# A trunk layer's first attention units: a PSUM strip for the scans, one projection bank, and stores behind the copies

## The chip, the cores and the metric

The kernel runs on one core of a Trainium2 chip. The metric is the device time of one execution in microseconds (us). In the profile PE is TensorE's matmul, PEld its weight load, DVE is VectorE, ACT ScalarE, POOL GpSimd; SP is the engine whose queue issues nearly all DMAs.

## What is computed

One decoder layer on x of 2048 tokens by 1024 features, float32: RMSNorm and a modulation by shift and scale, one input projection, attention on 16 heads of 64 (8 "stick-breaking", 8 "forgetting"), a per-head norm, an output projection, a gated residual, a gated MLP with a causal convolution, and a final RMSNorm. The change lies in the stick-breaking heads:

```
z = q.k / 8                      for s < t (strict)
A[t,s] = sigmoid(z_ts) * prod_{s<j<t} (1 - sigmoid(z_tj))
o = A v
```

The product runs from the diagonal back to s = 0, so a row of A is a running product read from right to left.

## The kernel before, in words

Tokens go in four blocks of 512 (`tb`), heads in pairs (`p`). A *unit* is one kind, one pair and one block; `units` lists 16 stick-breaking units and then 16 forgetting ones. Each unit has a projection (`proj_gen`, a generator advanced step by step by `fill_proj`) and an attention part (`attend`). Every float32 operand is split into a high part (ACT copy) and a low part (subtraction on DVE or POOL, `split`), and a product is three matmuls.

The first four units (pair 0, blocks 0 to 3) also normalise and modulate x. `first_block` does block 0; `norm_proj` does blocks 1 to 3 through `modulate`: four ACT squares (L95), a square root, four DVE multiplications (L108), then for each of eight feature tiles four PE transposes (L114), an affine step `hf`, and the split into `hp`. Each `hp` tile is stored to DRAM as `hs` (L433, 512 KB each) for the later pairs, which load it again (L321). A q accumulator `aq` and a k accumulator `ak` take 24 matmuls each (L252) in banks of tag `pj`, which has two banks in this stretch. `finish_proj` evacuates q (L262, L263) and k, copies them into `Q` and `K` by eight DMAs on SP (L266, L278), and makes V in four banks of 24 matmuls each (L247), of the same tag.

Attention part `SbItem.weights` makes the logits in PSUM (L442, L443), two sigmoids on ACT (L531 into `r`, L532 into `a`), a scan of `r` from right to left on DVE, and a multiplication on POOL (L546). `Group.turn` transposes the result and splits it (L457, L461, L462), `Group.add` multiplies it with V (L472). A row is cut into chunks of 512 keys, the last chunk first. The last chunk's scan (L538) stops products at the diagonal by a strip of constants, `edge`. Other chunks take the running product of the chunk to their right.

For units 0 to 2, `long_rows` is false. There each chunk has a tile of its own: POOL copies the neighbour's leftmost column into column `need` (L543) and the scan (L545) runs over 513 columns with initial value 1.0, both its inputs being `r` in SBUF. `edge` is read from SBUF. From unit 3 on, `long_rows` is true: pool `psa` is closed and opened again, one of its two banks becomes `edge_bank`, an ACT copy of `edge` into PSUM (L906), and tag `pj` has one bank; scans read that PSUM bank as second input and take the neighbour's column as the initial value (L541).

All loops are unrolled. The order on each engine is made by the framework's scheduler from the program order and modelled times; `tc.issue_after(ins)` keeps the instructions traced in its block behind `ins` on its engine. Attention of unit u stands in the program behind the projection of unit u, and between its steps stand those of projection u+1. x of block 1 is loaded in `first_block`, of block 2 behind `hs` of block 0 (L425), of block 3 when its projection starts. The list `first_done` holds instructions behind which the next `modulate` puts its squares and multiplications; before, only unit 0 fills it.

Of the kernel before, what the change touches and what calls it, by code (L numbers as in the profile page):

```python
# [11 lines left out]
AF = mybir.ActivationFunctionType  # L12
ALU = mybir.AluOpType
# [20 lines left out]
def kernel(ctx: ExitStack, tc: tile.TileContext, x, c, w_ada, b_ada, g_attn, w_in, b_fgate,  # L34
# [5 lines left out]
    def f(t):  # L40
        return t.bitcast(F32)
# [109 lines left out]
    def bank(pool, tag, bufs):  # L151
        return pool.tile([P, 512], F32, name=f"ps_{tag}", tag=tag, bufs=bufs)

    pj = lambda: bank(psa, "pj", 1 if edge_bank is not None else 2)
    qk = lambda: bank(psb, "qk", 2)
    pt = lambda: bank(psb, "pt", 3)
    pv = lambda: bank(psb, "pv", 1)
# [96 lines left out]
    def finish_proj(kind, p, tb, aq, w, hts, res, ak=None, avs=()):  # L254
        i = units.index((kind, p, tb))
        more = 3 < i < 16
        Q = ex.tile([P, 2, 2, TB], F32R, name="Q") if more and i % 3 == 2 else sb.tile([P, 2, 2, TB], F32R, name="Q", bufs=2)
        K = ex.tile([P, 2, TB], F32R, name="K") if i in (5, 13) else sb.tile([P, 2, TB], F32R, name="K", bufs=5)
        V = sb.tile([P, 4, 2, P], F32R, name="V", bufs=6)
        q2 = sl_.tile([P, 2, TB], F32R, name="q2", bufs=2)  # L260
        k2 = sl_.tile([P, 2, TB], F32R, name="q2", bufs=2)
        nc.scalar.activation(q2[:, 0], aq, AF.Copy, scale=-HD ** -0.5)  # L262
        nc.vector.scalar_tensor_tensor(q2[:, 1], aq, -HD ** -0.5, f(q2[:, 0]), ALU.mult, ALU.subtract)  # L263
        for h in range(2):
            for r in range(2):
                nc.sync.dma_start(f(Q[r * HD:(r + 1) * HD, h]), f(q2[h * HD:(h + 1) * HD]))  # L266
        if ak is None:
            ak = pj()
            for kt in range(KT):
                accumulate(ak, 1, w[0], hts[kt], kt)  # L270
                if kt % 2:
                    yield
        evacuated = split(k2[:, 0], k2[:, 1], ak, nc.vector)
        if i == 0:
            first_done.extend(evacuated)
        for h in range(2):
            for r in range(2):
                last_copy[:] = [nc.sync.dma_start(f(K[r * HD:(r + 1) * HD, h]), f(k2[h * HD:(h + 1) * HD, r])).ins]  # L278
        yield
        spill = vs[kind][p // 2][tb]  # L280
        if p % 2:
            nc.sync.dma_start(f(V), spill)
        else:
            V1 = (ex.tile([P, 4, 2, P], F32R, name="V") if (kind, p) == ("sb", 2) else
                  sb.tile([P, 4, 2, P], F32R, name="V", bufs=6))
            forget = (kind, p) == ("sb", 0)
            step, width = (1, 2 * P + NH) if forget else (2, 2 * P)
            if forget:
                zn = px.tile([P, 4, NH], F32, name="zn", bufs=1)
            for i in range(0, 4, step):  # L290
                if i < len(avs):
                    av = avs[i]
                else:
                    av = pj()
                    for t in range(step):
                        for kt in range(KT):
                            accumulate_v(av[:, t * width:(t + 1) * width], w[1], hts[kt], kt, i + t)
                            if kt % 4 == 3:
                                yield
                if forget:  # L300
                    nc.vector.tensor_copy(zn[:, i], av[:, 2 * P:width])
                av = av[:, 0:step * 2 * P].rearrange("p (t e h d) -> p t e h d", t=step, e=2, h=2)
                for e, v in enumerate((V, V1)):
                    v = v[:, i:i + step]
                    split(v[:, :, :, 0:HD], v[:, :, :, HD:P], av[:, :, e], nc.vector)
            if forget:
                b = pt()
                nc.tensor.transpose(b[0:4 * NH, 0:P], zn.rearrange("p t n -> p (t n)"), ident)
                zt = px.tile([4 * NH, P], F32, name="zt", bufs=1)
                nc.scalar.activation(zt, b[0:4 * NH, 0:P], AF.Identity, bias=bf_c)  # L310
                nc.sync.dma_start(zs[tb], zt)
            nc.sync.dma_start(spill, f(V1))
        res.append((Q, K, V))
        yield

# [19 lines left out]
    def first_block(xts, w, res):  # L335

        keep = tc.keep_in_program_order
        base = 3 * 512
        aq, ak = pj(), pj()
        avs = [qk(), qk(), pt()]  # L340
        junk = junk_x()
        for xt in xts:
# [28 lines left out]
        for kt in range(KT + 1):  # L371
# [42 lines left out]
            if kt + 1 < KT:  # L414
                with behind_last():
                    turned.append(turn(kt + 1))
        second_x.extend(load_x(1, keep))
        for t in range(4):
            keep(nc.sync.dma_start(bf_c[t * NH:(t + 1) * NH], b_fgate.rearrange("o n -> n o")))
        yield  # L420
        yield from finish_proj("sb", 0, 0, aq, w, hts, res, ak, avs)
        with tc.issue_after(last_copy[0]):
            for kt in range(KT):
                nc.sync.dma_start(hs[0][kt], f(hts[kt]))
            second_x.append(load_x(2))  # L425

    def norm_proj(tb, xts, w, res):
        aq = pj()
        hts = []

        def done(kt, h):
            hts.append(h)
            nc.sync.dma_start(hs[tb][kt], f(h))  # L433
            accumulate(aq, 0, w[0], h, kt)

        yield from modulate(px, pt, xts, mod_a, lambda kt: h_tile(), done, "a", nc.vector if tb == 1 else None, tb > 1,
                            junk_x())
        yield from finish_proj("sb", 0, tb, aq, w, hts, res)

    def logits(cw, qcols, hl, Q, K):  # L440
        b = qk()
# [60 lines left out]
    class SbItem:  # L502
# [14 lines left out]
        def weights(self, qi):  # L517
            head, ch = self.head, self.ch
            last = ch == head.n - 1
            need = min(512, (2 * head.j + qi + 1) * P - ch * 512)  # L520
            b = logits(max(need, 2 * P), head.qcols(qi), head.hl, head.Q, head.K[ch])
            if last:
                head.right = getattr(head, "right", [None, None])
                if long_rows:
                    head.right[qi] = sx.tile([P, S + 1], F32, name="rw", bufs=3)
            if long_rows:
                r = head.right[qi][:, ch * 512:ch * 512 + need + 1]
            else:
                r = sx.tile([P, 512 + 1], F32, name="r", bufs=7)
            self.at[qi] = a = sx.tile([P, 512], F32, name="a", bufs=7)  # L530
            nc.scalar.activation(r[:, :need], b[:, :need], AF.Sigmoid)  # L531
            nc.scalar.activation(a[:, :need], b[:, :need], AF.Sigmoid, scale=-1.0)  # L532
            if last:

                nc.gpsimd.memset(r[:, need:need + 1], 0.0)
                rev = r[:, 0:need][:, ::-1]
                strip = edge if edge_bank is None else edge_bank
                nc.vector.tensor_tensor_scan(rev, rev, strip[:, TB - need:TB][:, ::-1], 0.0, ALU.mult, ALU.max)  # L538
            elif long_rows:
                rev = r[:, 0:need][:, ::-1]  # L540
                nc.vector.tensor_tensor_scan(rev, rev, edge_bank[:, 0:need], r[:, need:need + 1], ALU.mult, ALU.bypass)  # L541
            else:
                nc.gpsimd.tensor_copy(r[:, need:need + 1], head.right[qi][:, 0:1])  # L543
                rev = r[:, 0:need + 1][:, ::-1]
                nc.vector.tensor_tensor_scan(rev, rev, rev, 1.0, ALU.mult, ALU.bypass)  # L545
            nc.gpsimd.tensor_mul(a[:, :need], a[:, :need], r[:, 1:need + 1])  # L546
            if not long_rows:
                head.right[qi] = r
# [204 lines left out]
        nc.vector.scalar_tensor_tensor(mod_m[:, 0], mod_m[:, 0], 1.0, cols[:, R_GM:R_GM + KT], ALU.add, ALU.mult)  # L753
        yield

    second_x = []
    last_copy = []
    units = [(k, p, tb) for k in ("sb", "fox") for p in range(4) for tb in range(NTB)]
    weights = {}
# [2 lines left out]
    def proj_gen(u, xts=None):  # L762
        kind, p, tb = u
        if tb == 0:
            weights[kind, p] = load_w(kind, p)
            results[kind, p] = []
        if u == units[0]:
            return first_block(xts, weights[kind, p], results[kind, p])
        if (kind, p) == ("sb", 0):
            return norm_proj(tb, second_x[:4] if tb == 1 else second_x[4] if tb == 2 else load_x(tb), weights[kind, p], results[kind, p])  # L770
        return proj(kind, p, tb, weights[kind, p], results[kind, p])

    HT = 2 * P
# [102 lines left out]
        yield from proj_gen(units[i], xt0 if i == 0 else None)  # L876

    psc = p2a = ex = edge_bank = None
    wo = []
    stock = [unit_proj(i) for i in range(len(units))]  # L880
    taken = [0]
# [18 lines left out]
    ex = open_pool("ex", side="right")  # L900
    sx = open_pool("sx", side="right")
    long_rows = True
    close_pool("psa")
    psa = open_pool("psa", side="right", space=PSUM)
    edge_bank = bank(psa, "edge", 1)
    nc.scalar.activation(edge_bank, edge[:, 0:TB], AF.Copy)  # L906
    base = taken[0]
    goal = 0
    seen = {}
# [11 lines left out]
        fill_proj(taken[0] + 1)  # L921
    close_pool("sx", "ex", "psa")
    ex = edge_bank = None
    psa = open_pool("psa", side="right", space=PSUM)
    sx = open_pool("fx", side="right")
    base = taken[0]
# [372 lines left out]
```

## Time and profile before

| what | value |
|---|---|
| median of 3 runs | 3098.84 us |
| the runs | 3099.03, 3098.84, 3090.37 us |
| the profiled execution's own time | 3090.19 us |
| its span | 3088.4 us |
| mean granted clock | 0.986 of full speed |
| PE busy | 2952.4 us, 96% |
| DVE, ACT, POOL busy | 2069.8, 1652.2, 1205.9 us |

The span is from the first to the last instruction; 1.8 us lie around it. A row of the windows view gives for one stretch its length and then busy us and instructions of each engine, the granted TensorE clock (1.00 is full speed), the share of time in which the 16 DMA engines were busy (rounded estimates can pass 1), and GB/s. A row grouped by line and form gives line, engine, operation, out<-in, shapes and count, then busy us, mean ns of one | idle us before the group and what ended it.

### The profile page before, as it was taken

What the parts mean: (1) busy time and instruction counts of PE and PEld (TensorE: products, weight loads), DVE (VectorE), ACT (ScalarE), POOL (GpSimd) and SP (SyncE); (2) the same over time, 40 slices, a digit from 0 to 9 for tenths busy, and PEclk for the clock granted to TensorE, in tenths of its full rate; (3) what the DMA queues carried; (4) which work ended last, traced back from release to release, by engine and by line L of the source; (5) the groups of instructions that cost most, each with busy time, mean ns of one, the idle gap of its engine ahead of it and who ended that gap; (6) DMA issues with size and microseconds to landing.
All of it is one profiled execution on the core that took longest, in us unless ns stands there. A gap on an engine that the chain in (4) does not pass through costs nothing.

```text
span 3088.4 us, 46309 instructions
## 1 busy us (share of the span) xinstructions
PE 2952.4 (96%) x15966; PEld 2507.9 (81%) x15966; DVE 2069.8 (67%) x3416; ACT 1652.2 (53%) x3041; POOL 1205.9 (39%) x1443
## 2 busy tenths in 40 slices
PE   6889999999999999999989899999899999999998
PEld 5778798989788888988878688888678888888887
DVE  5776788878856775657733777778977777254253
ACT  5665777767755655566634444444544444343332
POOL 1563655556531332242122344444444442332331
PEclk9999999999999999999999999999999999999999
DMA  8648634565166875595457532223332223565562
GB/s 234 214 137 266 194 116 148 179 198 164 26 221 219 292 225 176 177 329 133 155 188 231 186 90 82 82 82 89 113 95 82 83 82 114 196 199 167 183 205 79
DMA packets 292811, 496.51 MB, mean 161 GB/s; under 512 B 29336, under 2 KB 177552, under 8 KB 291552
## 3 DMA queue, kind: packets, MB, share of 16 engines
q1 hardware_dynamic: 280944, 480.92, 49.4%
q10 hardware_dynamic: 11632, 12.63, 1.2%
q8 instruction: 126, 2.06, 0.3%
q14 instruction: 109, 0.89, 0.1%
HBM read 352.61 MB, written 90.51 MB: 143 GB/s over the span
## 4 chain that ended last, share of the span: by engine, by line
PE 18%; DVE 10%; POOL 7%; DMA 7%; issue 5%; ACT 2%; SPq 1%; POOLq 0%; ACTq 0%; DVEq 0%
PE ps_o L1238 8%; PE ps_t L1238 4%; PE ps_bc L1238 4%; DMA wuraw<-in_w_up_dram 4%; DVE wu L45 3%; PE ps_o L1065 2%; POOL ws L1053 2%; POOL wuraw L1052 2%; DVE u L1134 2%; POOL ws L1051 2%; DMA hm<-hf_m 1%; DMA r<-rstd 1%; DVE u L1166 1%; DVE u L1133 1%; ACT wu L44 1%
## 5 line engine op out<-in xcount | busy, mean ns | idle before, releaser
L1065 PE MATMUL ps_o<-oa,wu 128*128 128x512 f32 x2088 | 504.5, 392 | 12.6 <-DVE oa L45 7.1
L1065 PEld LDWEIGHTS ps_o<-oa,wu 128*128 128x128 f32 x2088 | 391.1, 189 | 104.8 <-DVE oa L45 11.5
L472 PE MATMUL ps_pv<-at,V 128*128 128x256 f32 x2304 | 433.0, 298 | 13.9 <-DVE at L462 6.2
L462 DVE TENSOR_TENSOR at<-ps_pt,at 128x512 fp32r<-128x512 f32 (+1 forms) x576 | 365.4, 651 | 118.4 <-ACT at L461 115.7
L252 PE MATMUL ps_pj<-hp,w_qk 128*128 128x512 f32 x1536 | 417.4, 404 | 20.9 <-DMA hp<-hs 9.6
L461 ACT ACTIVATE at<-ps_pt 128x512 fp32r<-128x512 f32 (+1 forms) x576 | 319.2, 580 | 161.4 <-PE ps_pt L457 122.1
L472 PEld LDWEIGHTS ps_pv<-at,V 128*128 128x128 f32 x2304 | 340.3, 191 | 47.5 <-DVE at L462 14.8
L546 POOL TENSOR_TENSOR a<-a,rw 128x512 f32<-128x512 f32 (+2 forms) x272 | 262.8, 969 | 233.8 <-DVE rw L541 97.7
L252 PEld LDWEIGHTS ps_pj<-hp,w_qk 128*128 128x128 f32 x1536 | 277.2, 190 | 79.3 <-DMA hp<-hs 13.0
L45 DVE TENSOR_TENSOR wd<-wide,wd 128x1024 fp32r<-128x1024 f32 x88 | 117.3, 1339 | 249.6 <-ACT wd L44 227.5
L442 PE MATMUL ps_qk<-K,Q 128*128 128x512 f32 (+2 forms) x640 | 259.9, 407 | 16.0 <-ACT a L532 9.6
L45 POOL TENSOR_TENSOR g<-graw,g 128x512 fp32r<-128x512 f32 x82 | 139.3, 1702 | 296.8 <-ACT g L44 290.2
L1238 PE MATMUL ps_o<-wd,g 128*128 128x512 f32 x1040 | 249.3, 389 | 0.1
L1065 PE MATMUL ps_t<-ob,wu 128*128 128x512 f32 x984 | 242.0, 390 | 1.0 <-ACT hf_m L964 1.0
L443 PE MATMUL ps_qk<-K,Q 128*128 128x512 f32 (+2 forms) x640 | 237.1, 371 | 0.0
L44 ACT ACTIVATE wu<-wuraw 128x512 fp32r<-128x512 f32 x214 | 133.0, 626 | 184.1 <-PE ps_o L1065 115.3
L541 DVE TENSOR_TENSOR_SCAN rw<-rw,ps_edge 128x512 f32<-128x512 f32 x168 | 211.5, 1269 | 26.0 <-ACT rw L531 25.0
L1238 PEld LDWEIGHTS ps_o<-wd,g 128*128 128x128 f32 x1040 | 195.2, 188 | 41.1 <-DVE y L1184 0.5
L1065 PEld LDWEIGHTS ps_t<-ob,wu 128*128 128x128 f32 x984 | 184.9, 188 | 40.2 <-ACT hf_m L964 1.2
L247 PE MATMUL ps_pj<-w_v,hp 128*128 128x256 f32 (+1 forms) x1464 | 215.8, 289 | 0.7 <-DVE q L263 0.6
L247 PEld LDWEIGHTS ps_pj<-w_v,hp 128*128 128x128 f32 x1464 | 194.7, 191 | 7.0 <-DVE q L263 1.0
L457 PE MATMUL ps_pt<-edge,a 128*128 128x128 f32 x1088 | 183.8, 276 | 13.3 <-POOL a L546 6.2
(246 smaller groups left out, 5694.2 us busy)
## 6 DMA issues: line engine op xcount, KB each, us to landing
hp<-hs SPq DMA_DIRECT2D x224, 512.0 KB
wuraw<-in_w_up_dram SPq DMA_DIRECT2D x84, 512.0 KB
wide<-in_w_down_dram SPq DMA_DIRECT2D x84, 512.0 KB
Q<-q SPq DMA_DIRECT2D x128, 256.0 KB
g<-u SPq DMA_DIRECT2D x42, 512.0 KB
graw<-g SPq DMA_DIRECT2D x82, 256.0 KB
K<-q SPq DMA_DIRECT2D x128, 128.0 KB
hs<-hp SPq DMA_DIRECT2D x32, 512.0 KB
```

Source lines behind the costliest of these rows:

```text
L45: return [a.ins, (lo_engine or nc.gpsimd).tensor_sub(lo, src, f(hi)).ins]
L247: nc.tensor.matmul(acc, h[:, a, tok], w[kt][:, bb, 0:acc.shape[1]], start=kt == 0 and m == 0, stop=kt == KT - 1 and m == 2)
L252: nc.tensor.matmul(acc, w[kt][:, a, n], h[:, bb], start=kt == 0 and i == 0, stop=kt == KT - 1 and i == 2)
L442: nc.tensor.matmul(b[:, :cw], Q[:, hl, 0, qcols], K[:, hl, :cw], start=True, stop=False)
L443: nc.tensor.matmul(b[:, :cw], Q[:, hl, 1, qcols], K[:, hl, :cw], start=False, stop=True)
L461: nc.scalar.activation(at[:, 0, lo:], b[:, lo:], AF.Copy)
L462: nc.vector.tensor_sub(at[:, 1, lo:], b[:, lo:], f(at[:, 0, lo:]))
L472: nc.tensor.matmul(o[:, 0:2 * P], head.V[kt // 4][:, kt % 4, head.hl, :], rhs, start=self.first and kk == 0 and w == 0, stop=self.last and ...
L541: nc.vector.tensor_tensor_scan(rev, rev, edge_bank[:, 0:need], r[:, need:need + 1], ALU.mult, ALU.bypass)
L546: nc.gpsimd.tensor_mul(a[:, :need], a[:, :need], r[:, 1:need + 1])
L1065: nc.tensor.matmul(b, w[:, p, j], o[:, q], start=first and i == 0, stop=last and i == 2, skip_group_check=True)
L1238: nc.tensor.matmul(banks[t][n], g[:, a, t * P:(t + 1) * P], w[:, b, n * TB:(n + 1) * TB], start=k == 0 and i == 0, stop=k == NKD - 1 and i ...
```

## The change

- Tag `pj` has one bank from the start (`pj_bufs = 1`) and two only from the forgetting units on. The other bank is `ak` of unit 0; behind its evacuation it becomes `edge_bank`, filled by the ACT copy. Pool `psa` is no longer closed ahead of unit 3.
- In the short rows, L538 always reads `edge_bank`. In place of the POOL copy L543 there is a POOL memset of 1.0, and the scan reads `r` and one broadcast column of `edge_bank`, with the neighbour's leftmost column as initial value.
- `hs` of every block is stored by a new function `store_h`, behind the K copies of that block's unit; ahead of the eight stores it loads x of the block after next unit's start (blocks 2 and 3).
- Units 1 and 2 put the last V evacuations into `first_done` as well.

```diff
-    pj = lambda: bank(psa, "pj", 1 if edge_bank is not None else 2)
+    pj = lambda: bank(psa, "pj", pj_bufs)
@@ finish_proj
-                    split(v[:, :, :, 0:HD], v[:, :, :, HD:P], av[:, :, e], nc.vector)
+                    evacuated = split(v[:, :, :, 0:HD], v[:, :, :, HD:P], av[:, :, e], nc.vector)
...
             nc.sync.dma_start(spill, f(V1))
+            if 0 < units.index((kind, p, tb)) < 3:
+                first_done.extend(evacuated)
@@ first_block
-        aq, ak = pj(), pj()
+        nonlocal edge_bank
+        aq, ak = pj(), bank(psa, "edge", 1)
...
-        second_x.extend(load_x(1, keep))
+        next_x.append(load_x(1, keep))
...
-        yield from finish_proj("sb", 0, 0, aq, w, hts, res, ak, avs)
+        for k, _ in enumerate(finish_proj("sb", 0, 0, aq, w, hts, res, ak, avs)):
+            if k == 0:
+                edge_bank = bank(psa, "edge", 1)
+                nc.scalar.activation(edge_bank, edge[:, 0:TB], AF.Copy)
+            yield
+        store_h(0, hts)
+
+    def store_h(tb, hts):
         with tc.issue_after(last_copy[0]):
+            if 0 < tb < 3:
+                next_x.append(load_x(tb + 1))
             for kt in range(KT):
-                nc.sync.dma_start(hs[0][kt], f(hts[kt]))
-            second_x.append(load_x(2))
+                nc.sync.dma_start(hs[tb][kt], f(hts[kt]))
@@ norm_proj
             hts.append(h)
-            nc.sync.dma_start(hs[tb][kt], f(h))
             accumulate(aq, 0, w[0], h, kt)
...
-        yield from finish_proj("sb", 0, tb, aq, w, hts, res)
+        for k, _ in enumerate(finish_proj("sb", 0, tb, aq, w, hts, res)):
+            if k == KT // 2:
+                store_h(tb, hts)
+            yield
@@ SbItem.weights
-                strip = edge if edge_bank is None else edge_bank
-                nc.vector.tensor_tensor_scan(rev, rev, strip[:, TB - need:TB][:, ::-1], 0.0, ALU.mult, ALU.max)
+                nc.vector.tensor_tensor_scan(rev, rev, edge_bank[:, TB - need:TB][:, ::-1], 0.0, ALU.mult, ALU.max)
...
-                nc.gpsimd.tensor_copy(r[:, need:need + 1], head.right[qi][:, 0:1])
+                nc.gpsimd.memset(r[:, need:need + 1], 1.0)
                 rev = r[:, 0:need + 1][:, ::-1]
-                nc.vector.tensor_tensor_scan(rev, rev, rev, 1.0, ALU.mult, ALU.bypass)
+                nc.vector.tensor_tensor_scan(rev, rev, edge_bank[:, 0:1].to_broadcast([P, need + 1]),
+                                             head.right[qi][:, 0:1], ALU.mult, ALU.bypass)
@@ proj_gen and the main loop
-        return norm_proj(tb, second_x[:4] if tb == 1 else second_x[4] if tb == 2 else load_x(tb), ...)
+        return norm_proj(tb, next_x.pop(), ...)
...
-    close_pool("psa")
-    psa = open_pool("psa", side="right", space=PSUM)
-    edge_bank = bank(psa, "edge", 1)
-    nc.scalar.activation(edge_bank, edge[:, 0:TB], AF.Copy)
```

## Rows read from the trace of the kernel before

**Rows 1.** Windows of the first attention units, us from the span's start.

```profile
76.00:108.00 32.00, 29.36 (x172) 24.75 (x170) 20.27 (x33) 26.91 (x54) 8.95 (x19) 0.95 1.02 356
108.00:124.00 16.00, 13.81 (x83) 12.96 (x83) 9.47 (x20) 8.36 (x24) 5.89 (x12) 0.79 0.07 22
124.00:158.00 34.00, 29.53 (x179) 23.88 (x178) 28.29 (x35) 20.30 (x41) 29.46 (x33) 1.00 0.54 195
158.00:172.00 14.00, 14.00 (x118) 14.00 (x117) 4.99 (x15) 5.73 (x15) 0.35 (x2) 1.00 0.59 157
172.00:232.00 60.00, 47.69 (x266) 38.56 (x265) 52.29 (x61) 43.99 (x94) 53.23 (x60) 0.91 0.33 117
232.00:250.00 18.00, 18.00 (x153) 18.00 (x152) 9.91 (x22) 6.50 (x17) 6.79 (x9) 1.00 0.71 181
250.00:265.00 15.00, 13.04 (x58) 9.87 (x57) 2.26 (x6) 3.28 (x10) 1.77 (x6) 1.00 1.00 342
```

**Rows 2.** Groups by form on DVE, 76 to 258 us: short rows' scans.

```profile
L545 DVE TENSOR_TENSOR_SCAN r<-r 128x513 f32<-128x513 f32 x24 | 39.7, 1656 | 4.4 <-POOL r L543 3.6 <-ACT r L531 0.7
L538 DVE TENSOR_TENSOR_SCAN r<-r,edge 128x512 f32<-128x512 f32 x6 | 9.6, 1607 | 0.5 <-ACT r L531 0.5
```

**Rows 3.** Groups by form on DVE, 260 to 520 us: long rows' scans.

```profile
L541 DVE TENSOR_TENSOR_SCAN rw<-rw,ps_edge 128x512 f32<-128x512 f32 x72 | 91.0, 1271 | 14.1 <-ACT rw L531 13.5
L538 DVE TENSOR_TENSOR_SCAN rw<-rw,ps_edge 128x512 f32<-128x512 f32 x11 | 13.4, 1216 | 3.7 <-ACT rw L531 3.5
```

**Rows 4.** Groups by form on POOL, 76 to 258 us.

```profile
L546 POOL TENSOR_TENSOR a<-a,r 128x512 f32<-128x512 f32 x30 | 40.2, 1346 | 11.7 <-DVE r L545 10.3 <-ACT r L531 1.2 <-ACT a L532 0.2
L45 POOL TENSOR_TENSOR hp<-hf_a,hp 128x512 fp32r<-128x512 f32 x16 | 22.7, 1422 | 0.0
L543 POOL COPY r<-r 128x1 f32<-128x1 f32 x24 | 12.4, 515 | 0.0
L45 POOL TENSOR_TENSOR w_qk<-raw_qk,w_qk 128x256 fp32r<-128x256 f32 x8 | 10.5, 1309 | 0.0
L535 POOL MEMSET r<- 128x1 f32 x21 | 1.8, 96 | 0.0
```

**Rows 5.** Groups by form on POOL, 260 to 520 us.

```profile
L546 POOL TENSOR_TENSOR a<-a,rw 128x512 f32<-128x512 f32 x82 | 91.4, 1115 | 92.1 <-DVE rw L541 47.6 <-ACT a L532 14.8 <-ACT at L461 11.5
L45 POOL TENSOR_TENSOR w_qk<-raw_qk,w_qk 128x256 fp32r<-128x256 f32 x8 | 5.8, 737 | 5.3 <-ACT w_qk L44 5.3
```

**Rows 6.** Timeline of PE: start us, us, instructions [idle before <-releaser].

```profile
108.55 0.36 PE L442 MATMUL ps_qk<-K,Q 128*128 128x256 f32 x1 [2.03 <-DMA K<-q]
...
158.61 6.10 PE L247 MATMUL ps_pj<-w_v,hp 128*128 128x264 f32 x48
...
172.33 0.28 PE L442 MATMUL ps_qk<-K,Q 128*128 128x256 f32 x1
...
180.73 0.79 PE L442 MATMUL ps_qk<-K,Q 128*128 128x512 f32 x1 [3.15 <-ACT a L532]
...
248.93 0.28 PE L442 MATMUL ps_qk<-K,Q 128*128 128x256 f32 x1
...
256.29 0.96 PE L252 MATMUL ps_pj<-hp,w_qk 128*128 128x512 f32 x3 [0.31 <-DMA hp<-hs]
258.66 5.73 PE L252 MATMUL ps_pj<-hp,w_qk 128*128 128x512 f32 x24 [1.41 <-DVE q L263]
```

**Rows 7.** Timeline of ACT.

```profile
169.17 1.06 ACT L95 ACTIVATE at<-xt 128x1024 f32<-128x1024 f32 x1 [3.12 <-issue]
...
178.30 1.28 ACT L531 ACT_TABLE_LOAD   x1
...
250.75 0.57 ACT L906 ACTIVATE ps_edge<-edge 128x512 f32<-128x512 f32 x1
```

**Rows 8.** Timeline of SP's queue.

```profile
162.40 2.93 SPq L278 DMA_DIRECT2D K<-q  x3
```

**Rows 9.** Waits of SP's queue, 40 to 275 us: total us, times, longest.

```profile
SPq L433 <- POOL r L535: 24.3, 3, 16.8
```

More of the change, by code (lines that the diff above doesn't have):

```diff
@@ L754, in late_mod @@
         yield
-    second_x = []
+    next_x = []
     last_copy = []
@@ L769, in proj_gen @@
         if (kind, p) == ("sb", 0):
-            return norm_proj(tb, second_x[:4] if tb == 1 else second_x[4] if tb == 2 else load_x(tb), weights[kind, p], results[kind, p])
+            return norm_proj(tb, next_x.pop(), weights[kind, p], results[kind, p])
         return proj(kind, p, tb, weights[kind, p], results[kind, p])
@@ L878 @@
     psc = p2a = ex = edge_bank = None
+    pj_bufs = 1
     wo = []
@@ L923 @@
     ex = edge_bank = None
+    pj_bufs = 2
     psa = open_pool("psa", side="right", space=PSUM)
```

## The prediction

> **What bounds the kernel now.** Over the whole span PE is busy 96% of the time, so I looked first for the stretch where it is not, in the 40 slices of the page (the first four slices are the low ones), and then cut the time from unit 0's attention to unit 4's projection into seven windows [rows 1]. I name them A to G in that order. Their bounds are my choice, at the points where the kind of work changes. In B, D and F the V matmuls of units 1, 2 and 3 run, in A, C and E an attention unit beside the next block's modulation and its q and k. PE is full only in D and F; in C it lacks 34.0 - 29.5 = 4.5 us and in E 60.0 - 47.7 = 12.3 us. What is late there is POOL (53.2 of 60 us in E, 29.5 of 34 in C) with DVE just behind (52.3 and 28.3). In D, F and G it is the other way round: DVE and POOL have little to do because the next unit's attention has not begun. After 265 us the change alters no operation; there I expect only what a shifted start does to it.
>
> The groups by form say why POOL and DVE are so full. The short rows' scan takes 1.656 us and the last chunk's 1.607 us for 512 columns [rows 2]; the same lengths against the PSUM strip take 1.271 and 1.216 us later on [rows 3]. POOL's multiplication takes 1.346 us here and 1.115 us there, its weight subtraction 1.309 against 0.737 us, and a copy of one column 0.515 us beside a memset of one column at 0.096 us [rows 4, 5]. So the operations of both engines are long where both read SBUF, and short where the scan's second input is PSUM.
>
> **The change, part by part.**
>
> *Scans and copies.* DVE saves 24 x (1.656 - 1.271) = 9.2 us and 6 x (1.607 - 1.216) = 2.3 us, 11.5 us in all [rows 2, 3]. POOL saves 24 x (0.515 - 0.096) = 10.1 us on the copies, 30 x (1.346 - 1.115) = 6.9 us and 8 x (1.309 - 0.737) = 4.6 us [rows 4, 5], 21.6 us. By the number of chunks two thirds of the first-mentioned scans and of the copies belong to unit 2 (16 of 24; unit 1 has 8, unit 0 none) and the last chunks are spread evenly, so E gets 6.1 + 0.8 = 6.9 us of DVE and 6.7 + 4.6 + 4.6 = 15.9 us of POOL. E then holds POOL 37.3, DVE 45.4, ACT 44.0 us. Its pacing engine was full to 53.2/60 = 0.89; DVE at that density would need 51 us, 9 us less, and what PE lacks (12.3 us) is the upper end. But ACT is nearly as long as DVE, and orders are fixed in advance; I take **-8 us**, between 0 and -12. The hop over POOL between two scans (3.6 us of DVE's waits [rows 2]) goes too and is part of this.
>
> [...]
>
> *C and the squares.* In C, POOL loses 3.4 + 2.3 = 5.7 us and DVE 3.1 + 0.8 = 3.9 us. But block 2's four squares now stand behind unit 1's last V evacuation, and so in unit 1's attention: 4 x 1.06 us, and two table loads of 1.28 us on ACT between sigmoids [rows 7], 6.8 us on an engine that has 20.3 in C [rows 1]. Behind them wait the sigmoids, and behind those the logits banks. The same thing happens today in unit 2, and there PE waited 3.15 us for L532 [rows 6]. One stall of that size against a gain of 3 to 4.5 us: **0**, between -4.5 and +5. For block 3 the squares only move by as much as V(2) ends later.
>
> *One projection bank.* Today `ak` runs beside `aq` tile by tile. With one bank it must wait until q is evacuated. Unit 4 has this already: the last `aq` matmuls begin at 256.29, `ak` has 1.41 us of idle PE ahead of it and takes 5.73 us [rows 6]. So k, its copies and the next attention are 7.1 us further behind `aq`, and V's four banks (about 3 us of matmuls each by [rows 6], 48 in 6.10 us) come one by one with their evacuations between. What hides it: in A the 5.7 us leave a nearly full PE (29.4 of 32 us), so `aq` ends earlier, and the 2.03 us wait for K's copy behind stores goes (next part): I take -1 for A and B. In D, K's last copies were issued by 165.3 us [rows 8] but the next logits ran at 172.33 [rows 6], 7 us later, since V stood ahead of them on PE; with one bank part of V can run under the next attention: 0. In F, where PE is full, 5.7 us more of matmuls go in, but logits that today begin at 248.93 [rows 6] can slip in between V's banks: +4. Sum **+3 us**. The ends: three times the whole 7.1 us, +21, if nothing hides it; and -10 if attention 2 and 3 each start 5 us earlier between V's banks.
>
> *Stores and x.* Eight stores of 512 KB per block leave the modulation and go behind the K copies. SP's queue loses its waits for `hp` (16.8 us in one of them, 24.3 in three [rows 9]), behind which weight loads and x stood. In A the DMA engines were fully busy, which is what K's copies queued behind (2.03 us, counted above). x of block 2 comes some 25 us later, but its squares wait for V(1) in any case. In E the stores go out of the way of nothing (share 0.33). In F and G they meet unit 4's loads: 4.2 MB at G's 342 GB/s are 12.3 us; F has 0.29 x 18 = 5.2 us free, so up to 7 us could be pushed into G [rows 1]. But the loads need tiles that V(3) frees only at its end. I take **+1 us**, between 0 and +7.
>
> *The strip.* One ACT copy of 0.57 us [rows 7] moves from a time when ACT is idle (3.3 of 15 us in G) to just behind unit 0's k, ahead of block 1's squares: **+0.6 us**. The pool that is no longer closed costs nothing now: unit 4's `aq` starts at F's end.
>
> *Clock.* [...] If K's copy no longer makes PE wait, some of B's 3.4 us (0.21 x 16) comes back: **-1 us**, between -3 and 0; a new stall in C would take as much.
>
> Sum: -8 + 0 + 3 + 1 + 0.6 - 1 = **-4.4 us**. From the profiled execution's 3090.2 us that gives 3085.8. Its time lies at the low end: two of three runs shown were near 3099 and one at 3090, the mean of these four executions is 3094.6. I put the shift there: 3094.6 - 4.4 = **3090 us**. About 0.3%, 9.3 us, is what a measurement of this kernel can tell from no change.
>
> **The rivals.**
>
> 1. *Attention starts between V's banks.* With one bank PE has gaps of an evacuation between V's banks, and the order may fill them with the next unit's logits as it did in B, so that DVE and POOL, idle in D and F, begin 5 us earlier twice: the bank term is -10 in place of +3, the sum -17.4, **3077 us**. For it: both engines have under 10 of 18 us in F. Against it: V also has to be there before the first L472.
> 2. *The bank holds everything up.* q, then k, then V, each through one bank, at each of three units; the place is the time from `aq`'s end to the next unit's first logits. It decides if these logits come more than about 5 us later than today's behind `aq` in each unit. Two thirds of 21 us, 14, in place of 3: sum +6.6, **3101 us**; with C's stall and G's push at their ends +5 and +7, +18, 3112 us. For it: unit 4's row shows the wait as it is, with DVE at 2.3 of 15 us meanwhile [rows 1, 6]. Against it: unit 2 had 7 us of slack.
> 3. *The scans do not get shorter.* If the broadcast column makes a PSUM scan as long as today's, only the copies go, E gains about 3 us and the sum is near 0, **3095 us**. Against it: the later rows' scans, with a whole PSUM row, are very even.
>
> [...]
>
> **How the numbers follow.** Forecast 0.40 (its own range 3084 to 3096), rival 1 0.28, rival 2 0.24, rival 3 0.08. Faster by over 0.3% are rival 1 and a fifth of the forecast: 0.36. Slower by over 0.3% are most of rival 2, 0.21. The rest, 0.43, is within 0.3%. The range for 8 in 10 goes from 3074 (rival 1 and a little more) to 3107 (the middle of rival 2's two ends).
>
> **What would show it.** Right: scans at 1.27 us in the short rows, POOL's copies gone and its multiplications near 1.1 us, unit 2's stretch 6 to 10 us shorter, `ak` as 24 matmuls in a row behind an evacuation in units 1 to 3. Wrong: scans above 1.4 us; unit 2's stretch as long as now with ACT as releaser; the first logits of units 1 to 3 over 5 us later behind `aq`; or unit 4's loads late by more than 5 us. A difference that arises after 265 us would be outside this account.

## The result, and the profile after

| | before | after |
|---|---|---|
| median (8 runs each) | 3091.47 us | 3111.49 us |
| range | 3089.67 to 3099.03 | 3107.07 to 3126.34 |
| profiled execution, span | 3090.19, 3088.4 | 3117.48, 3115.7 |

The ratio is 1.0067 (95% interval 1.0048 to 1.0086): slower by 20 us. The forecast was 3090 us. The time is that of rival 2 with C's stall and G's push at their ends (3112 us). Every trace, here and below, is of one execution, and some lie well above their median: 3117.48 us here, 3111.31 in run 4 (median 3101.20), 3077.96 in run 17 (median 3067.34).

The windows A to G of [rows 1] for the changed kernel (length; busy us of PE, PEld, DVE, ACT, POOL; clock; DMA share; GB/s):

```profile
76.00:108.00 32.00, 27.01 (x149) 20.32 (x147) 18.23 (x32) 20.69 (x47) 8.79 (x22) 1.00 0.56 171
108.00:124.00 16.00, 13.57 (x85) 12.04 (x84) 8.68 (x15) 5.98 (x17) 5.19 (x13) 0.89 0.95 362
124.00:158.00 34.00, 25.73 (x155) 21.59 (x155) 24.11 (x37) 26.39 (x51) 21.12 (x28) 0.85 0.04 17
158.00:172.00 14.00, 13.63 (x91) 12.18 (x89) 5.71 (x12) 4.62 (x12) 0.70 (x4) 1.00 0.64 150
172.00:232.00 60.00, 47.93 (x287) 40.68 (x287) 44.27 (x64) 43.87 (x91) 33.95 (x56) 0.91 0.37 135
232.00:250.00 18.00, 15.93 (x112) 14.70 (x113) 8.18 (x17) 8.47 (x19) 7.07 (x10) 1.00 0.69 189
250.00:265.00 15.00, 11.10 (x87) 10.47 (x86) 3.34 (x12) 2.64 (x9) 1.76 (x6) 1.00 0.98 340
```

In 124 to 158 us POOL is no longer late (21.1 us and 28 operations in place of 29.5 and 33), and yet PE does less: 25.7 us at a clock of 0.85 in place of 29.5 at 1.00. The pacing engine of before got shorter and PE idles more. The windows are fixed in time, so where a unit's end has moved they no longer hold quite the same work.

The groups by form, DVE and POOL, 76 to 272 us (busy us, mean ns | idle ahead), beside [rows 2, 4]:

```profile
L557 DVE TENSOR_TENSOR_SCAN r<-r,ps_edge 128x513 f32<-128x513 f32 x24 | 30.0, 1270 | 2.7 <-ACT r L544 1.1 <-issue 1.1 <-POOL r L555 0.5
L550 DVE TENSOR_TENSOR_SCAN r<-r,ps_edge 128x512 f32<-128x512 f32 x6 | 7.3, 1210 | 0.4 <-ACT r L544 0.4
...
L559 POOL TENSOR_TENSOR a<-a,r 128x512 f32<-128x512 f32 x30 | 33.1, 1106 | 27.3 <-ACT a L545 13.5 <-DVE xt L108 7.2 <-DVE r L557 2.9
L45 POOL TENSOR_TENSOR w_qk<-raw_qk,w_qk 128x256 fp32r<-128x256 f32 x8 | 5.7, 732 | 9.7 <-ACT w_qk L44 9.7
```

These are the prices of the forecast to within 1%. The loss is in PE's timeline (start, us, instructions [idle before <-releaser]), beside [rows 6]:

```profile
95.99 5.75 PE L252 MATMUL ps_pj<-hp,w_qk 128*128 128x512 f32 x24
103.16 3.20 PE L247 MATMUL ps_pj<-w_v,hp 128*128 128x264 f32 x24 [1.41 <-DVE q L45]
106.19 0.28 PE L455 MATMUL ps_qk<-K,Q 128*128 128x256 f32 x1
...
119.41 4.68 PE L247 MATMUL ps_pj<-w_v,hp 128*128 128x264 f32 x24 [1.90 <-DVE V L45]
...
135.03 0.66 PE L114 MATMUL ps_pt<-edge,xt 128*128 128x128 f32 x2 [5.71 <-DVE xt L108]
...
167.58 3.10 PE L247 MATMUL ps_pj<-w_v,hp 128*128 128x264 f32 x24
...
171.00 0.28 PE L455 MATMUL ps_qk<-K,Q 128*128 128x256 f32 x1
...
180.39 4.71 PE L247 MATMUL ps_pj<-w_v,hp 128*128 128x264 f32 x24
...
186.72 3.18 PE L247 MATMUL ps_pj<-w_v,hp 128*128 128x264 f32 x24 [1.62 <-DVE V L45]
...
200.64 0.48 PE L114 MATMUL ps_pt<-edge,xt 128*128 128x128 f32 x1 [5.62 <-DVE xt L108]
...
243.58 3.20 PE L247 MATMUL ps_pj<-w_v,hp 128*128 128x264 f32 x24 [1.93 <-DVE q L45]
248.84 0.37 PE L455 MATMUL ps_qk<-K,Q 128*128 128x256 f32 x1
...
263.48 0.28 PE L308 MATMUL ps_pt<-edge,zn 128*32 128x128 f32 x1 [0.26 <-DVE zn L301]
```

`ak` is 24 matmuls in a row behind `aq`, as foretold. The first logits of units 1 to 3 run at 106.19, 171.00 and 248.84 us, not later than before (108.55, 172.33, 248.93 in [rows 6]), since they slip in between V's banks. Counted from the end of `aq`, as rival 2 asked, they come 11.6, 12.2 and 18.6 us behind it (9.1, 15.0 and 19.6 before, where `ak` ends with it): 2.5 us later at most. But V's four banks of unit 2 now take from 167.58 to 189.9 us, 22 us, where 13.7 us were enough before (158.61 to 172.3, [rows 6]). Some rows of DVE show why, first of the kernel after, then of the kernel before:

```profile
177.07 0.29 DVE L45 TENSOR_TENSOR V<-ps_pj,V 128x128 fp32r<-128x128 f32 x1 [0.34 <-ACT V L44]
177.70 2.46 DVE L557 TENSOR_TENSOR_SCAN r<-r,ps_edge 128x513 f32<-128x513 f32 x2 [0.34 <-ACT r L544]
180.07 0.26 DVE L45 TENSOR_TENSOR V<-ps_pj,V 128x128 fp32r<-128x128 f32 x1
```

```profile
162.33 0.29 DVE L45 TENSOR_TENSOR V<-ps_pj,V 128x128 fp32r<-128x128 f32 x1 [0.35 <-ACT V L44]
162.97 0.29 DVE L45 TENSOR_TENSOR V<-ps_pj,V 128x128 fp32r<-128x128 f32 x1 [0.34 <-ACT V L44]
```

Now two scans of the attention that has begun stand between the two halves of one bank's evacuation, and the next V bank starts only at 180.39 us. Logits stand between V's banks on PE too, and the third bank's matmuls took 4.71 us in place of 3.1, at a granted clock of 0.76 (179 to 186 us).

Behind V's last evacuation stand the next block's squares, and PE runs dry for 5.6 to 5.7 us twice. L308, the transpose behind the last V bank, is my mark for a unit's end. For units 1 to 3 it stood at 121.42, 172.81 and 249.89 us before and stands at 124.35, 190.16 and 263.48 us now: +2.9, +17.4, +13.6 us. From mark to mark unit 2 takes 14.4 us more and unit 3 3.8 us less; part of attention 2 has run between V's banks by then.

ACT in the first dry stretch:

```profile
126.16 0.25 ACT L44 ACTIVATE V<-ps_pj 128x128 fp32r<-128x128 f32 x1
126.31 1.04 ACT L95 ACTIVATE at<-xt 128x1024 f32<-128x1024 f32 x1
...
131.13 1.06 ACT L95 ACTIVATE at<-xt 128x1024 f32<-128x1024 f32 x1
132.09 0.19 ACT L95 ACTIVATION_READ_ACCUMULATOR at<-xt 128x1 f32 x1
132.29 1.28 ACT L96 ACT_TABLE_LOAD   x1
133.59 0.30 ACT L96 ACTIVATE ss_a<-ss_a,epsc 128x4 f32<-128x4 f32 x1
133.91 1.28 ACT L545 ACT_TABLE_LOAD   x1
136.16 0.60 ACT L545 ACTIVATE a<-ps_qk 128x512 f32<-128x512 f32 x1 [0.97 <-PE ps_pt L470]
```

From V's last evacuation on ACT to the next sigmoid of a full chunk behind the table loads it is 9.7 us; PE's 5.7 dry us lie in it, and end with DVE's L108, which waits for the square root at 133.59 us. POOL's next multiplication starts at 136.89 us, as L108's 2.74 us end (136.87), and the 7.2 us ahead of it are those that the group's row above puts to L108; but its own input leaves ACT at 136.76 us, so these rows do not show whether L108 held POOL up.

### The profile page after: what moved, and what is told of

Read it like the earlier page. It is cut to its first block, busy times and chain, and to the rows that moved or that the text cites. A ratio compares the mean times of both kernels' runs of the same rounds, so it can differ in the third digit from the quotient of the medians.

```text
span 3115.7 us, 46303 instructions
## 1 busy us (share of the span) xinstructions
PE 2960.1 (95%) x15966; PEld 2511.9 (81%) x15966; DVE 2062.6 (66%) x3416; ACT 1653.5 (53%) x3041; POOL 1178.4 (38%) x1443
## 4 chain that ended last, share of the span: by engine, by line
PE 56%; DVE 13%; DMA 12%; POOL 6%; issue 6%; ACT 5%; SPq 1%; POOLq 0%; ACTq 0%; DVEq 0%
PE ps_pj L252 9%; PE ps_o L1249 8%; PE ps_pv L485 6%; PE ps_pj L247 6%; PE ps_pt L470 5%; PE ps_o L1076 4%; PE ps_t L1249 4%; PE ps_bc L1249 4%; DMA wuraw<-in_w_up_dram 3%; PE ps_qk L455 3%; PE ps_qk L456 3%; DVE wu L45 2%; DMA hp<-hs 2%; POOL ws L1064 2%; PE ps_t L1076 2%
## 5 line engine op out<-in xcount | busy, mean ns | idle before, releaser
L252 PE MATMUL ps_pj<-hp,w_qk 128*128 128x512 f32 x1512 | 413.4, 406 | 13.6 <-DMA hp<-hs 12.3
L553 DVE TENSOR_TENSOR_SCAN rw<-rw,ps_edge 128x512 f32<-128x512 f32 x168 | 211.8, 1270 | 36.9 <-ACT rw L544 35.9
L247 PEld LDWEIGHTS ps_pj<-w_v,hp 128*128 128x128 f32 x1464 | 195.5, 192 | 21.1 <-issue 7.3
L44 ACT ACTIVATE wd<-wide 128x1024 fp32r<-128x1024 f32 x88 | 92.6, 1057 | 192.9 <-PE ps_bc L1249 186.6
```

Of the source, the lines that this page charges most:

```text
L44: a = nc.scalar.activation(hi, src, AF.Copy)
L247: nc.tensor.matmul(acc, h[:, a, tok], w[kt][:, bb, 0:acc.shape[1]], start=kt == 0 and m == 0, stop=kt == KT - 1 and m == 2)
L252: nc.tensor.matmul(acc, w[kt][:, a, n], h[:, bb], start=kt == 0 and i == 0, stop=kt == KT - 1 and i == 2)
```

## Experiments

Each was timed in five rounds beside the kernel before; that kernel's median moved between 3089 and 3095 us from one set to the next, so the ratios are what to compare; where the intervals of two of them overlap, the text says so. Edits are against the kernel named; "the mark" is L308 of unit 3 (249.89 us before, 263.48 after).

**1. The squares' order.** After, without the new `first_done` entries:

```diff
-            if 0 < units.index((kind, p, tb)) < 3:
-                first_done.extend(evacuated)
```

> The changed kernel without the two new entries in first_done: block 2's and 3's squares no longer stand behind the V evacuation. Theory S (squares): the two idle stretches of PE, 5.7 us at 129 to 135 us and 5.6 us at 195 to 200 us of the changed kernel, and the lower clock behind each, go; 12 to 16 us less than the changed kernel, some 3097 us, +6 over before. Theory B (one bank): the time lies in k and V going through one bank one after the other; 0 to 4 us less than the changed kernel, some 3109 us, and V of unit 3 still ends 12 us or more later than before.

3102.98 us, ratio 1.0046 (1.0029 to 1.0063), mark at 256.88. By the ratios some 6 us of the 20 belong to this edit, and the mark is 6.6 us earlier; the two intervals overlap, so the time alone does not show it. The 5.7 us stalls are gone, but V stays slow (units 1 and 2 end at 128.7 and 191.1 us): with the squares ahead, V's evacuation is what PE waits for.

```profile
123.31 5.17 PE L247 MATMUL ps_pj<-w_v,hp 128*128 128x264 f32 x24 [5.07 <-DVE V L45]
```

**2. The bank alone.** Before, with `pj_bufs = 1` in units 1 to 3; the other bank holds unit 0's k and then the strip, as in the change, but short rows do not read it. Nothing else of the change.

> The kernel before with one projection bank in units 1 to 3 (the other bank becomes the strip's from unit 0 on) and nothing else: short scans, copies, stores and squares as before. Theory B: 14 to 21 us more than before, 3105 to 3112 us, most of it at unit 3, where k's 24 matmuls and V's four banks follow aq one by one. Theory S: 0 to 4 us more than before, since PE is short of work in that stretch anyway.

3113.64 us, ratio 1.0083 (1.0063 to 1.0104), +25 us; mark at 267.84. The bank by itself is worse than the whole change.

**3. The bank and the scans.** As 2, with the scans and the memset of the change.

> The kernel before with one projection bank and the new scans on the PSUM strip; stores and squares as before. Theory B: the bank costs 14 to 21 us and the scans give back 8, so 3097 to 3104 us, 6 to 8 us below the run with the bank alone. Theory S: 4 to 8 us less than before, some 3085 us.

3109.68 us, ratio 1.0060 (1.0044 to 1.0076); mark at 260.69. The scans give back 7 us by the ratio (the intervals overlap; the medians are 4 us apart) and 7 us at the mark.

**4. The stores and x alone.** Before, with `store_h` for all blocks behind the K copies.

> The kernel before with the stores of h and the loads of x behind the K copies (two banks, old scans, first_done as before). Theories S and B: within 4 us of before, 3088 to 3095 us, with K's copy of unit 1 no longer waited for (2 us). A third, D (DMA): the stores of block 3 push unit 4's loads, and the time is 5 us or more above before.

3101.20 us, ratio 1.0038 (1.0024 to 1.0053), +12 us: three times the 4 us that theories S and B allowed, and in the range of D, whose wait is there too (2.73 us for `hp` ahead of unit 4's q). ACT:

```profile
110.69 1.06 ACT L95 ACTIVATE at<-xt 128x1024 f32<-128x1024 f32 x1 [4.04 <-DMA xt<-in_x_dram]
...
115.02 1.06 ACT L95 ACTIVATE at<-xt 128x1024 f32<-128x1024 f32 x1 [2.13 <-DMA xt<-in_x_dram]
```

Block 2's squares wait for x on ACT, V's evacuations and the sigmoids stand behind them, and from 116 to 132 us the granted clock is 0.57 (0.97 before).

**5. Stores behind K, x of block 2 where it was.** Against run 4:

```diff
-            if 0 < tb < 3:
-                next_x.append(load_x(tb + 1))
+            if tb == 2:
+                next_x.append(load_x(3))
             for kt in range(KT):
                 nc.sync.dma_start(hs[tb][kt], f(hts[kt]))
+            if tb == 0:
+                next_x.append(load_x(2))
```

> The kernel before with h's stores behind the K copies, two projection banks, old scans; but x of block 2 is loaded where it was before, behind block 0's stores, and only x of block 3 moves. Theory X (late x): the 12 us that stores and x cost together came from ACT, whose squares waited for x of block 2 with V's evacuation queued behind; then this takes 8 to 14 us less than that run, 3087 to 3093 us. Theory D (the stores themselves: they meet unit 4's loads, or hold h's tiles): the time stays within 4 us of that run, some 3100 us.

3099.97 us beside 3092.56, ratio 1.0022 (1.0013 to 1.0032). By the ratios about 5 of the 12 us were x and 7 are the stores; the two intervals overlap. Two lines of PE show one reason, and a claim of mine that fell:

```profile
105.45 0.36 PE L451 MATMUL ps_qk<-K,Q 128*128 128x256 f32 x1 [1.96 <-DMA K<-q]
...
253.56 4.83 PE L252 MATMUL ps_pj<-hp,w_qk 128*128 128x512 f32 x12 [2.90 <-DMA hp<-hs]
```

K's wait (2.03 us in [rows 6]) is still there with no store of block 1 ahead of the copies. And unit 4's first matmuls wait for `hp`, because block 3's stores run into its loads.

**6. Block 3's stores where they were.** As 5, but `tb == 3` stores each tile as it is made.

> The kernel before with h's stores of blocks 1 and 2 behind the K copies, block 3's at once as before, x of block 2 as before; two banks, old scans. Theory G (block 3's eight stores push unit 4's loads): the 7 us of the run with x early go, 3088 to 3093 us, and PE no longer waits near 3 us for hp. Theory T (stores behind the copies hold h's tiles, which costs in every block): 3096 us or more.

3094.04 us, ratio 1.0012 (1.0002 to 1.0022); no wait for `hp` above 0.32 us. So the wait of 2.9 us was block 3's stores; in the time they are worth 3 us by the ratios, whose intervals overlap.

**7. The form of the scan alone.** Before, with memset, initial value and broadcast column, but read from `edge` in SBUF.

```diff
-                nc.gpsimd.tensor_copy(r[:, need:need + 1], head.right[qi][:, 0:1])
+                nc.gpsimd.memset(r[:, need:need + 1], 1.0)
...
-                nc.vector.tensor_tensor_scan(rev, rev, rev, 1.0, ALU.mult, ALU.bypass)
+                nc.vector.tensor_tensor_scan(rev, rev, edge[:, 0:1].to_broadcast([P, need + 1]),
+                                             head.right[qi][:, 0:1], ALU.mult, ALU.bypass)
```

> The kernel before with the new form of the short scan (a memset of 1.0, the neighbour as initial value, a broadcast column as second input), but that column is read from edge in SBUF; two banks, stores and squares as before. Theory P (the PSUM source shortens them): scans stay near 1.6 us on the mean and vary from 1.2 to 2.3 us, POOL's multiplications stay near 1.35 us; time 0 to 4 us below before. Theory F (the form does it): scans fall to 1.27 us and the time 5 us or more below before.

3088.85 us, ratio 0.9992 (0.9979 to 1.0005): no difference that can be told.

```profile
L550 DVE TENSOR_TENSOR_SCAN r<-r,edge 128x513 f32<-128x513 f32 x24 | 40.7, 1706 | 3.8 <-POOL a L552 1.5 <-POOL r L548 1.1 <-ACT r L536 0.9
...
L552 POOL TENSOR_TENSOR a<-a,r 128x512 f32<-128x512 f32 x30 | 40.5, 1354 | 14.9 <-DVE r L550 12.4 <-ACT r L536 2.3
```

The copies are gone and nothing else changed: with both inputs in SBUF the scan stays at 1.7 us and POOL's multiplication at 1.35 us. It is the PSUM source, not the form: 1.706 us with the column in SBUF, 1.270 us with it in PSUM in the changed kernel.

The means do not say whether two SBUF inputs are slow in themselves. Single scans of the kernel before do; each is shown with POOL's rows about it:

```profile
112.92 1.23 DVE L545 TENSOR_TENSOR_SCAN r<-r 128x513 f32<-128x513 f32 x1 [0.89 <-POOL r L543]
114.29 1.09 POOL L546 TENSOR_TENSOR a<-a,r 128x512 f32<-128x512 f32 x1 [1.38 <-DVE r L545]
...
142.19 2.27 DVE L545 TENSOR_TENSOR_SCAN r<-r 128x513 f32<-128x513 f32 x1 [0.57 <-POOL r L543]
142.10 1.28 POOL L45 TENSOR_TENSOR hp<-hf_a,hp 128x512 fp32r<-128x512 f32 x1
143.32 1.12 POOL L543 COPY r<-r 128x1 f32<-128x1 f32 x1
```

The three scans of this form that ran with POOL idle took 1.21 to 1.23 us, no more than the PSUM form. Beside POOL's work, in whole or in part, the others took 1.21 to 2.28 us, and the copy of one column shown here 1.12 us in place of 0.19. So the long ones are found only where the two engines work side by side; with a PSUM source both are short on the mean there (1.27 and 1.11 us in the changed kernel).

**8. A PSUM source without a bank.** Before, with the second sigmoid written back into the logits' own bank; the short rows' scans read it there and `edge` from SBUF, and POOL's copy is off the path.

```diff
+                nc.scalar.activation(a[:, :need], b[:, :need], AF.Sigmoid, scale=-1.0)
+                nc.scalar.activation(b[:, :need], b[:, :need], AF.Sigmoid)
...
+                nc.vector.tensor_tensor_scan(rev, b[:, 0:need][:, ::-1], edge[:, 0:need],
+                                             head.right[qi][:, 0:1], ALU.mult, ALU.bypass)
```

> The kernel before with scans of the short rows that read PSUM without costing a bank: the second sigmoid is written back into the logits bank and the scan reads it there, with edge in SBUF as second input and the neighbour as initial value (the POOL copy of the column stays, off the scan's path). Two banks, stores and squares as before. Theory B (the strip is good, its bank is what costs): scans of 1.3 us, POOL as in the changed kernel, 4 to 9 us below before, some 3083 us. Theory Q: the logits banks stay taken until the scan has read them, PE waits longer for L442, and the time is that of before or up to 6 us more.

3081.41 us, ratio 0.9968 (0.9958 to 0.9978), -10 us; mark at 238.08. One row each of DVE, POOL and the windows:

```profile
L555 DVE TENSOR_TENSOR_SCAN r<-ps_qk,r,edge 128x512 f32<-128x512 f32 x24 | 30.6, 1279 | 11.7 <-ACT ps_qk L541 11.7
...
L557 POOL TENSOR_TENSOR a<-a,r 128x512 f32<-128x512 f32 x30 | 33.1, 1106 | 17.0 <-DVE r L555 12.2 <-DVE var L655 2.9 <-DVE r L548 1.4
...
172.00:232.00 60.00, 57.02 (x347) 49.52 (x348) 47.70 (x68) 44.16 (x92) 40.75 (x62) 0.89 0.45 141
```

With both banks kept and scans as short, PE is busy for 57.0 us of E in place of 47.7; E now also holds a part of unit 3's V, which before began at 232.13 us.

**9. k elsewhere.** After, with `ak` of units 1 to 3 in a bank of the transposes' tag: `ak = pt() if 0 < i < 4 else pj()`.

> The changed kernel, but k of units 1 to 3 is accumulated in a bank of tag pt, so that it may run beside q; V still goes through the one bank of tag pj. Theory K (k behind q is the larger part of the bank's cost): 10 us or more less than the changed kernel, 3100 us or below, and V of unit 3 ends 8 us or more earlier. Theory V (V's four banks one by one are the larger part): 0 to 5 us less, 3106 to 3111 us, with PE idle 1.3 to 1.9 us ahead of V's banks as in the changed kernel.

3109.44 us, ratio 1.0060 (1.0046 to 1.0073); mark at 261.11. By the ratios k's place is worth 2 us, which the intervals do not tell from nothing. k runs beside q again, but then PE waits for K's copies (3.75 us at 106.86 us).

**10. Every second V bank elsewhere.** After, with

```diff
-                    av = pj()
+                    av = pt() if tb and (kind, p) == ("sb", 0) and i % 2 else pj()
```

> The changed kernel, but every second bank of V of units 1 to 3 is of tag pt, so V's four banks alternate between two; k stays behind q in the one bank of tag pj. Theory V (V's banks one by one are the larger part of the bank's cost): 8 us or more less than the changed kernel, about 3102 us or below, V of unit 3 ends 8 us or more earlier. Theory K (k behind q is the larger part): 0 to 4 us less.

3095.07 us beside 3091.37, ratio 1.0016 (1.0007 to 1.0026); mark at 244.38. 16 of the 20 us go with V's banks taking turns again; here the intervals are clear of each other. What is left beside the mark is a wait of unit 4:

```profile
252.09 2.50 PE L252 MATMUL ps_pj<-hp,w_qk 128*128 128x512 f32 x5 [4.77 <-DMA hp<-hs]
```

**11. Both.** Edits 9 and 10 together.

> The changed kernel with both: k of units 1 to 3 and every second bank of V in tag pt. If the one bank is the whole of what the change costs beyond squares and stores, this takes away most of it: 12 to 18 us less than the changed kernel, 3093 to 3099 us. If tag pt's banks are as scarce as tag pj's (the transposes of the attention unit and of the modulation use them), it takes 0 to 6 us less.

3091.20 us, ratio 1.0000 (0.9991 to 1.0010). The whole loss is gone, but the 10 us of run 8 are not there. Against run 10, k's place is worth about 5 us here (the intervals touch).

**12 to 16. What swallows them.** Each starts from 11: without the `first_done` entries (12), with block 3's stores early (13), with x of block 2 early (14), with x early and no entries (15), all three (16).

> The change with k and every second V bank of units 1 to 3 in a bank of the transposes' tag, as in the run that came out at 1.0000 of before, and without the first_done entries of units 1 and 2 (squares free again to run ahead of the last V evacuation). Two other single edits of this case measured the squares' order at 6 to 8 us and the shorter scans at 10 us. Theory A (the order of the squares swallows the scans' gain once the banks are given back): 6 to 8 us below before, ratio 0.9975. Theory B (the stores of block 3 behind K's copies swallow it): no change against before, ratio 0.999 to 1.001. If both are wrong, the transposes' bank that V borrows is what costs, and the ratio is 1.000 as well, with stalls of PE ahead of the transposes.

> The change with k and every second V bank of units 1 to 3 in a bank of the transposes' tag, first_done entries kept, and block 3's eight stores issued as each tile is made, as before the change; blocks 1 and 2 stay behind the K copies. Theory B (block 3's stores meet the loads of unit 4, which made PE wait 2.7 to 4.8 us there): 3 to 5 us below before, ratio 0.9985, and the wait of PE for hp ahead of unit 4's q under 1 us. Theory A (the squares' order swallows the gain): ratio 1.000, with two stalls of PE of over 5 us behind V of units 1 and 2 left as they are.

> The kernel with k and every second V bank of units 1 to 3 in a bank of the transposes' tag, at 1.0000 of before, and x of block 2 loaded where it was before the change (in front of the K copies' stores of the block before, not behind unit 1's K copies). Theory C (late x, whose squares stand on ACT ahead of attention 1's sigmoids until 119 to 122 us, swallows the scans' 10 us): ratio 0.997 to 0.9985, and the granted clock of 116 to 132 us, 0.57 in that kernel, above 0.9. With the squares still tied to V's last evacuation the gain may stop at 3 us. Against C: ratio 1.000 and the clock low as it was; then V, which ends at 114 us and no longer fills the opening of attention 1, is what swallows it.

> As the last one, without the first_done entries of units 1 and 2. Theory C: x there and its squares free, 7 to 10 us below before, ratio 0.9972, clock of 116 to 132 us above 0.9. Against C: ratio 1.000 to 1.002, as with late x.

> As the last one, with block 3's stores issued as each tile is made: of the change, only the strip, the scans and the stores of blocks 1 and 2 behind K's copies are left. Theory C: 8 to 13 us below before, ratio 0.9965. If the stores of blocks 1 and 2 and the scans work together here as they did in the kernel that read the scan's input from the logits bank, 20 us below, ratio 0.9935. Against C: ratio 1.000.

| run | median us | ratio (95%) | clock 116 to 132 us | mark, us against before | store at 931 us, against before |
|---|---|---|---|---|---|
| 11 | 3091.20 | 1.0000 (0.9991, 1.0010) | 0.57 | -0.3 | +3.4 |
| 12 | 3099.93 | 1.0019 (1.0010, 1.0028) | 0.62 | -2.8 | -2.7 |
| 13 | 3094.69 | 0.9998 (0.9984, 1.0012) | 0.68 | -0.3 | -0.9 |
| 14 | 3089.79 | 0.9996 (0.9984, 1.0008) | 0.68 | -4.3 | +1.8 |
| 15 | 3089.75 | 0.9990 (0.9978, 1.0001) | 0.80 | -5.5 | -4.5 |
| 16 | 3089.92 | 0.9996 (0.9984, 1.0008) | 0.83 | -6.4 | -8.5 |

No combination is faster than before by more than its interval; the gains of 3 to 13 us that a theory of each run expected did not come. Run 12 is slower than before, by 5 to 6 us, where 6 to 8 us less had been expected: with the banks given back, taking out the `first_done` entries alone costs about 6 us against run 11 (the intervals touch), and with x early (15 against 14) it makes no difference. Inside the trace the edits do add up: the store of the attention output that ran at 930.8 us before (an `oT` store of SP) moves from +3.4 to -8.5 us. But in the profiled execution of 16 only 1.8 us of it are left at the last such store. Where the rest goes between 930 us and the end is open.

One stretch differs from run 8 throughout: V is done by 112 to 114 us (119.1 us in run 8), when attention 1 is just opening, and then PE has little beside logits that wait for sigmoids (1.5 to 4 us each time). The window 116 to 132 us of run 11 and then of run 8:

```profile
116.00:132.00 16.00, 11.21 (x40) 8.77 (x40) 11.93 (x19) 13.45 (x30) 7.11 (x15) 0.57 0.81 329
```

```profile
116.00:132.00 16.00, 15.47 (x100) 13.04 (x99) 12.84 (x21) 11.06 (x26) 10.97 (x16) 0.98 0.26 100
```

40 against 100 matmuls. That V is needed as filler there is read from these rows and was not tried by itself. Nor was the other difference: in runs 11 to 16 k and V borrow banks of the transposes' tag.

**17. The version to keep.** Run 8's scans with run 6's stores (blocks 1 and 2 behind the K copies, block 3 at once, x early), two banks:

> The scan that reads the logits bank, with h's stores of blocks 1 and 2 behind the K copies and block 3's at once, x of block 2 as before, x of block 3 ahead of block 2's stores. If these stores are worth anything once they no longer meet unit 4's loads: 2 to 5 us below the run with the logits bank alone, some 3078 us; if not, within 2 us of it, some 3082 us.

3067.34 us (3065.28 to 3077.96), ratio 0.9927 (0.9914 to 0.9940): 24 us faster than before, 44 faster than after; mark at 229.99.

```profile
108.00:172.00 64.00, 57.33 (x380) 51.26 (x379) 43.19 (x76) 42.63 (x96) 30.50 (x52) 0.93 0.54 188
172.00:232.00 60.00, 59.86 (x406) 54.30 (x405) 47.35 (x71) 43.17 (x93) 41.21 (x67) 0.97 0.61 199
```

PE is busy for 59.9 of E's 60 us; V of unit 3 now lies in E as a whole. The stores that cost 3 to 4 us by themselves (run 6) gain 13 here by the ratios (0.9927 against 0.9968), beside short scans; why they do so with the scans of run 8 and not with those of run 16 was not isolated.

## Why the prediction was wrong

- *One projection bank*: the step that failed. Stated +3 us, "if nothing hides it" +21; measured +25 alone (run 2), and 20 go when k and V get their turns back (11). The working priced k's 7.1 us and let V run under the next attention at nothing. k is worth 2 us (9) to 5 us (11 against 10), V's banks 16 (10). They do run under the attention, as I wrote, but there a bank waits for an evacuation that stands among sigmoids and scans on ACT and DVE (in run 1 among squares too), so V needs 22 us in place of 13.7 in unit 2, and the next block's work waits for V's end. Rival 2's time came, but not at its place: it was to be decided by the first logits, and these were at most 2.5 us later behind `aq`. Its 3112 us is a hit of the number by luck. What happened in order was rival 1, with the other sign.
- *Squares*: stated 0, with an end of +5; about +6 (1), not clear of noise. I took one stall of 3 us; there were two of over 5, since with one bank V's last evacuation comes 3 to 17 us later and there is no work left beside them. With the banks given back the same entries cost nothing: without them the time was about 6 us longer (12 against 11).
- *Stores and x*: stated +1, with an end of +7; alone +12, of which x some 5, block 3's stores 3 and the other stores about 4. The push into G came there (2.9 us of wait). But neither wait is in the changed kernel: its squares start right behind V's last evacuation (126.31 us) without a wait for x, as the prediction had it, and no wait of unit 4 for `hp` is above 0.39 us. Runs 1 and 3, which differ in stores and x alone beside one bank, are 4 us apart the other way (the intervals overlap). So the parts do not add up: 25 - 7 + 12 + 6 = 36 against 20 measured. That x's squares wait for V(1) "in any case" holds only with the new entries (run 4). Wrong was that K's wait comes from the stores of block 1 (1.96 us without them).
- *Scans and copies*: stated -8; measured -7 with one bank (3 against 2) and -10 with two (8). Right in price and, as far as the intervals tell, in size. Rival 3 is out.
- *Strip* (+0.6) and *clock* (-1) were not measured apart; the strip's copy is part of run 2, and no run shows the clock's -1 us. What the traces show is that the clock fell in C (0.85 for 1.00; 0.51 from 136 to 140 us, behind the first dry stretch) and rose in B (0.89 for the 0.79 from which the 0.21 x 16 was taken).
- *After 265 us* no difference was expected. The shift is +13.6 us at the mark, +17.0 at 931 us and +25.7 at the last of those stores, in one execution each. It grows from 14 to 20 us about 710 us and from 18 to 30 us about 1270 us; in the four stretches of 20 us from 1230 us the granted clock was 0.86, 1.00, 0.92 and 0.91, and 1.00 throughout before. What starts that is not explained, and half of the loss in these two executions lies behind the mark.

## What to carry to other kernels

Here a bank of an accumulate-and-evacuate pair was worth what its evacuations wait on the busiest stretch (V's turns 16 us, k's 2 to 5), not what they last when the engines are idle: price each accumulation that goes through it, V's four as well as k's one. Before giving a bank to constants so that a scan has a PSUM source, look for one that is there already: the logits' own bank did it without taking one from k and V, and gained 10 us (run 8). And work that "can run under" the next phase has a cost if something else waits for its end: V of unit 2 took 22 us there in place of 13.7, and the next block's work waited.

## What the runs showed of the hardware

A VectorE scan of two SBUF inputs of 512 or 513 columns took 1.61 to 1.74 us on the mean of a form beside POOL's work (before and run 7), single ones 1.21 to 1.23 us with POOL idle and up to 2.28 us beside its work (before); with one input in PSUM it took 1.21 to 1.28, whichever of the two inputs that was (runs 3 and 8). POOL's multiplication went from 1.35 us (before and run 7) to 1.11 us with it (after and run 8), and a POOL copy of one column from 0.52 us (before) to 0.19 us (run 8).
